# One tile form for the compressed branch and the row-maxima product, and separate PSUM banks and weight buffers for the second half's gated product

## The chip, the cores and the metric

The kernel runs on one core of one Trainium2 chip. The metric is device time in microseconds of one execution, as the median of several executions. The engines have short names here: PE is TensorE's matrix multiply and PEld its weight load, DVE is VectorE, ACT is ScalarE, POOL is GpSimd, SP is SyncE, which issues the DMA transfers.

## What is computed

One layer of a hybrid model over 1024 tokens of width 1024. Cut to what matters here:

```python
h = _rms_norm(x, norm_mix)
u = h @ w_in                      # queries, three kinds of keys and values, gates, RWKV inputs, merge gates
# attention: 8 heads in 2 groups; three branches are summed with gates:
#   compressed: 63 keys, each made of 32 tokens (mask: 16 n + 31 <= t)
#   selected:   causal over all 1024 tokens (16 blocks of 64, top 16 of 16)
#   window:     the last 512 tokens
o_nsa = gate0 * o_cmp + gate1 * o_slc + gate2 * o_win
o_rwkv = _rwkv7(...)              # a recurrence over the tokens, 8 heads
y = sig(merge0) * (o_nsa @ proj_nsa) + sig(merge1) * (o_rwkv @ proj_rwkv)
x = x + y @ w_out
x = x + _conv_ffn(_rms_norm(x, norm_ffn), ffn_up, ffn_conv, ffn_down)
```

## The kernel before

The tokens are cut into two halves of 512 columns. A dense product runs in two parts: weights and inputs are split into a high part and a rest (`whi`, `wlo`, `xhi`, `xlo`), and `mm3` adds three matmuls for each 128 input rows, 24 matmuls of 512 columns for a product of 1024 rows and 12 for one of 512. `wload` (L211) brings the weights: a DMA into `wraw`, a copy to `whi` on ACT (L216) and a subtraction to `wlo` on POOL (L217), two buffers of each. PSUM has four pairs of banks, called P, M, A and B, and `ps(tag)` takes the two of a pair in turn.

The program has four stages. (1) The input norm. (2) Attention with all projections of `u`: the attention of a head runs at its own pace, and dense products (the fillers `zproj`, `mproj`) are put between its steps, with small matmuls that prepare the RWKV part (`prelude`, L794, `loraproj`, L821). (3) The RWKV recurrence, with fillers again: the first half's `nproj`, `rproj`, `wout0`, `norm0` and `ffn0`. (4) The second half: `gated` for its eight output tiles (L1208 to L1215), then `w_out`, the norm, and the feed-forward part. A scheduler writes the order of each engine's instructions when the program is built, by priorities and its own estimate of durations; every engine then runs its list in order.

Attention of a head (`i`, `g`) goes in three steps. Row maxima are found for the three branches and put into `mx`, for all 1024 tokens. They are needed on the partitions of `q2`, beside the query's rest, so they go through a product with the identity: `M` holds, per token, three maxima and their rests, and the matmul of L500 turns 128 tokens of it into rows of PSUM. Then for each branch and half, L528 and L530 make scores with the keys on the partitions, L532 adds a mask, ACT takes the exponential twice (L537, L538), DVE the rest (L539), and L542, L545 and L547 multiply with the values. In the compressed branch the keys are 64 (63 and one empty), so its matmuls use a part of the array. Last, the finished heads are turned (L566), copied by ACT into `oT` (L568) and stored (L569).

A matmul's tile form is the part of the array that it uses, rows by columns. The trace shows it behind the tiles' names: `128*128` is the whole array, `128*64` half of its columns (64 outputs), `64*128` half of its rows (64 inputs), `64*64` a quarter.

In stage 4, `gated(m, 1, ...)` makes one 128x512 output tile: DVE multiplies the product with the gate (L652), POOL adds it to `yt` (L653), ACT and DVE split the sum into `yhi` and `ylo` (L1214, L1215). The products of `w_out` read all eight tiles of those.

## Time and profile before

| | |
|---|---|
| median of 3 runs | 1892.82 us (1892.15 to 1898.71) |
| profiled execution, its own time | 1890.38 us |
| span of the profiled execution, first to last instruction | 1888.6 us |
| PE busy | 1826.6 us (97%) |
| DVE, ACT, POOL busy | 980.8, 797.7, 655.6 us |
| attention with its fillers | about 130 to 660 us |
| the second half's gated products | 1164 to 1188 us |

How to read it: a row of the timeline gives the start of an instruction and its duration. Matmuls are pipelined, so a duration holds time in which the next ones already run; how much a matmul costs is read from one start to the next. A PE that is busy by the table can still be slowed from within.

### The profile page before, as it was taken

To read this page: it belongs to the slowest core of one execution; us is meant where nothing else is said; L and a number is where in the kernel's file an instruction comes from. 1 tells how busy PE (TensorE), PEld (TensorE's weight loads), DVE (VectorE), ACT (ScalarE), POOL (GpSimd) and SP (SyncE) were. 2 spreads that over 40 slices of the span, in tenths; PEclk is the share of its full clock that TensorE was granted. 3 is DMA by queue.
4 is the path that set the end of the run, shared out by engine and by line. 5 is a ranking of instruction groups with operands and counts; after the bars stand their busy time and mean duration, and the time that the engine had idled before them with its cause. 6 is when DMAs were issued, how large, how long until landed. Compare 5 with 4: busy or idle time off the path is not lost.

```text
span 1888.6 us, 30480 instructions
## 1 busy us (share of the span) xinstructions
PE 1826.6 (97%) x12106; PEld 1418.5 (75%) x12106; DVE 980.8 (52%) x1775; ACT 797.7 (42%) x1434; POOL 655.6 (35%) x412
## 2 busy tenths in 40 slices
PE   8999999999999999999999799999999999999998
PEld 5985656666777788777777588778888888888886
DVE  6214666767766404863443444265666553444444
ACT  5243765656566523454564443344222222222211
POOL 5212042132233434112155345756444433313220
PEclk9999999999999999899999899999999999999999
DMA  5425142232333336254544544425222211111102
GB/s 176 119 61 186 29 163 85 82 121 58 114 126 124 129 135 230 96 174 157 198 136 136 166 132 157 144 104 204 89 78 90 81 59 56 45 34 59 42 12 89
DMA packets 121342, 211.23 MB, mean 112 GB/s; under 512 B 23664, under 2 KB 52720, under 8 KB 120944
## 3 DMA queue, kind: packets, MB, share of 16 engines
q1 hardware_dynamic: 121200, 209.29, 33.4%
q8 instruction: 95, 1.56, 0.3%
q14 instruction: 47, 0.39, 0.1%
HBM read 151.00 MB, written 53.48 MB: 108 GB/s over the span
## 4 chain that ended last, share of the span: by engine, by line
PE 81%; DVE 8%; DMA 4%; issue 3%; ACT 3%; POOL 1%; SPq 0%; POOLq 0%; DVEq 0%; ACTq 0%
PE psP L223 29%; PE psA L223 12%; PE psM L223 9%; PE psP L1301 6%; PE psB L1301 6%; PE psA L528 1%; PE psA L390 1%; PE psA L530 1%; DVE pl L539 1%; PE psM L997 1%; PE psM L475 1%; DVE mp L481 1%; PE psP L821 1%; DVE hf L205 1%; PE psB L542 1%
## 5 line engine op out<-in xcount | busy, mean ns | idle before, releaser
L217 POOL TENSOR_TENSOR wlo<-wraw,whi 128x1024 fp32r<-128x1024 f32 (+1 forms) x154 | 346.6, 2252 | 577.8 <-ACT whi L216 173.0
L223 PE MATMUL psP<-hhi,whi 128*128 128x512 f32 x816 | 335.2, 412 | 16.5 <-ACT hhi L702 9.9
L223 PE MATMUL psP<-hlo,whi 128*128 128x512 f32 x816 | 330.7, 406 | 3.2 <-DVE hlo L703 1.8
L216 ACT ACTIVATE whi<-wraw 128x1024 fp32r<-128x1024 f32 (+1 forms) x154 | 152.4, 990 | 222.8 <-PE psP L223 84.7
L223 PE MATMUL psP<-hhi,wlo 128*128 128x512 f32 x816 | 215.6, 398 | 0.0
L223 PEld LDWEIGHTS psP<-hhi,whi 128*128 128x128 f32 x816 | 156.8, 193 | 56.2 <-ACT hhi L702 11.9
L223 PEld LDWEIGHTS psP<-hlo,whi 128*128 128x128 f32 x816 | 156.8, 192 | 40.4 <-DVE hlo L703 3.4
L223 PEld LDWEIGHTS psP<-hhi,wlo 128*128 128x128 f32 x816 | 152.5, 190 | 33.6 <-issue 0.7
L539 DVE TENSOR_TENSOR pl<-pf,ph 128x512 f16<-128x512 f32 (+4 forms) x208 | 123.5, 602 | 44.3 <-ACT pf L538 43.4
L537 ACT ACTIVATE ph<-psA 128x512 f16<-128x512 f32 (+4 forms) x208 | 98.8, 475 | 79.5 <-PE psA L532 57.7
L481 DVE TENSOR_REDUCE mp<-psM 128x1 f32<-128x512 f32 (+1 forms) x192 | 94.4, 513 | 42.2 <-PE psM L479 34.2
L1288 POOL TENSOR_TENSOR dl<-draw,dh 128x1024 fp32r<-128x1024 f32 x22 | 53.6, 2452 | 155.9 <-ACT dh L1287 96.7
L1265 DVE SCALAR_TENSOR_TENSOR u<-psA,par,u 128x511 f32<-128x511 f32 x64 | 47.7, 746 | 99.8 <-ACT u L1261 99.4
L538 ACT ACTIVATE pf<-psA 128x512 f32<-128x512 f32 (+4 forms) x208 | 99.3, 477 | 0.0
L1303 DVE TENSOR_TENSOR x<-x,psP 128x512 f32<-128x512 f32 x88 | 60.2, 684 | 68.1 <-PE psP L1301 67.7
L1287 ACT ACTIVATE dh<-draw 128x1024 fp32r<-128x1024 f32 x22 | 22.3, 1054 | 151.5 <-PE psB L1301 148.2
L1303 DVE TENSOR_TENSOR x<-x,psB 128x512 f32<-128x512 f32 x88 | 60.2, 684 | 45.1 <-PE psB L1301 45.1
L1265 DVE SCALAR_TENSOR_TENSOR u<-psM,par,u 128x511 f32<-128x511 f32 x64 | 47.7, 746 | 64.0 <-ACT u L1261 63.7
L1282 POOL TENSOR_TENSOR hl<-th,hh 128x1024 fp32r<-128x1024 f32 x22 | 52.8, 2402 | 74.6 <-ACT hh L1281 74.6
L542 PEld LDWEIGHTS <-ph 128*128 128x128 f16 (+1 forms) x592 | 55.7, 96 | 23.2 <-issue 10.9
L547 PEld LDWEIGHTS <-pl 128*128 128x128 f16 (+1 forms) x592 | 55.3, 98 | 22.9 <-DVE pl L539 8.0
L1301 PE MATMUL psP<-hh,dh 128*128 128x512 f32 x176 | 69.0, 392 | 2.1 <-ACT hh L1281 2.1
(377 smaller groups left out, 4254.5 us busy)
## 6 DMA issues: line engine op xcount, KB each, us to landing
wraw<-f_up SPq DMA_DIRECT2D x68, 512.0 KB, 3.2
wraw<-w_t SPq DMA_DIRECT2D x46, 512.0 KB, 3.5
draw<-f_dn SPq DMA_DIRECT2D x22, 512.0 KB, 3.2
sg_d<-zs SPq DMA_DIRECT2D x32, 256.0 KB, 2.0
wraw<-w_out SPq DMA_DIRECT2D x16, 512.0 KB, 3.3
z_d<-zs SPq DMA_DIRECT2D x28, 256.0 KB, 2.2
x<-xT SPq DMA_DIRECT2D x24, 256.0 KB, 5.8
zs<-sg_d SPq DMA_DIRECT2D x24, 256.0 KB, 3.0
```

What stands on the lines that cost most here:

```text
L216: A.activation(hi[:, :nk], raw, AF.Copy)
L217: G.tensor_sub(lo[:, :nk], raw, hi[:, :nk].bitcast(F32))
L223: T.matmul(ps, a[:, k], ks_(b, k), start=(n == 0), stop=(n == 3 * nk - 1))
L481: V.reduce_max(mp[:, x, br, t:t + 1], pm[:, 0:(b1 - b0) * 128], axis=AX.X)
L537: A.activation(ph[0:nkey, rg], pa[0:nkey, rg], AF.Exp, scale=0.125)
L538: A.activation(pf[0:nkey, rg], pa[0:nkey, rg], AF.Exp, scale=0.125)
L539: V.tensor_sub(pl[0:nkey, rg], pf[0:nkey, rg], ph[0:nkey, rg])
L542: T.matmul(pov[:, t, :], ph[0:nkey, tk], vt[0:nkey, kb, g, 0:65], start=first, stop=False, skip_group_check=True)
L547: T.matmul(pov[:, t, :], pl[0:nkey, tk], vt[0:nkey, kb, g, 0:65], start=False, stop=True, skip_group_check=True)
L1265: V.scalar_tensor_tensor(u[:, e0 + d:e0 + 512], pj[:, 0:512 - d], cw_, u[:, e0 + d:e0 + 512], op0=ALU.mult, op1=ALU.add)
L1301: T.matmul(pj, a[:, m], b[:, H[h]], start=(n == 0), stop=(n == 3 * len(hd_) - 1))
L1303: V.tensor_add(x2[m][:, H[h]], x2[m][:, H[h]], pj)
```

## The change

Three things are edited.

1. The compressed branch's keys, values, mask and scores are padded from 64 to 128 keys (`kcn`, `kch`, `kcl`, `Vc`, `k1c`, `k2c`, `mcT`, `nkey`). The padded keys are zero and masked. `M` gets 128 columns instead of 64 and holds its six columns at `oth.start`, so that L500 fills all 128 partitions of PSUM and the maxima still land where ACT reads them (L502). All matmuls of these lines then have the form 128*128. The count of instructions stays.
2. `oT` gets one buffer instead of two.
3. The second half's `gated` takes the bank pair B instead of P, and its weights come through buffers of their own (`whi`, `wlo`, `wraw` of four tiles of 128 columns, two buffers each, in the pool `op`). The first half's `gated` keeps P and the common buffers.

```diff
--- before.py
+++ after.py
@@ -118,8 +118,7 @@
     mdT = np.where(key > tok, NEG, 0.0)
     meT = np.where(key <= tok, NEG, 0.0)
     n64 = ar(64)
-    mcT = np.where(16 * n64[:, None] + 31 > ar(S)[None, :], NEG, 0.0)
-    mcT = np.concatenate([mcT, mcT], 0)
+    mcT = np.where(16 * p[:, None] + 31 > ar(S)[None, :], NEG, 0.0)
     mc = mcT[:64].T.reshape(8, 128, 64).transpose(1, 0, 2).reshape(128, 512)
     s64, t64 = p[:, None] % 64, n64[None, :]
     gm = np.concatenate([s64 < t64, s64 <= t64], 1)
@@ -208,10 +207,12 @@
 
         lastw = [None]
 
-        def wload(src, nk):
-            hi = wp.tile([128, 8, 128], FR, name="whi", bufs=2)
-            lo = wp.tile([128, 8, 128], FR, name="wlo", bufs=2)
-            raw = wp.tile([128, 8, 128], F32, name="wraw", bufs=2)[:, :nk]
+        def wload(src, nk, pool_=None):
+            t_ = pool_ or wp
+            n = nk if pool_ else 8
+            hi = t_.tile([128, n, 128], FR, name="whi", bufs=2)
+            lo = t_.tile([128, n, 128], FR, name="wlo", bufs=2)
+            raw = t_.tile([128, n, 128], F32, name="wraw", bufs=2)[:, :nk]
             lastw[0] = load(raw, src).ins
             A.activation(hi[:, :nk], raw, AF.Copy)
             G.tensor_sub(lo[:, :nk], raw, hi[:, :nk].bitcast(F32))
@@ -265,7 +266,7 @@
 
         Vs = ap_.tile([128, 8, 2, 130], F16, name="Vs")
         Vw = ap_.tile([128, 8, 2, 130], F16, name="Vw")
-        Vc = ap_.tile([64, 1, 2, 130], F16, name="Vc")
+        Vc = ap_.tile([128, 1, 2, 130], F16, name="Vc")
         G.memset(Vs[:, :, :, 64:65], 1.0)
         G.memset(Vw[:, :, :, 64:65], 1.0)
         G.memset(Vc, 0.0)
@@ -301,7 +302,7 @@
 
         WT = D["w_t"]
         kst1, kst2 = {}, {}
-        for nm, n in (("s", S), ("w", S), ("c", 64)):
+        for nm, n in (("s", S), ("w", S), ("c", 128)):
             for g in range(2):
                 kst1[nm, g] = ap_.tile([128, n], F16, name=f"k1{nm}{g}")
                 kst2[nm, g] = ap_.tile([128, n], F16, name=f"k2{nm}{g}")
@@ -334,7 +335,7 @@
                 for g in range(2):
                     for kv in range(2):
                         load(cw2[64 * g:64 * g + 64, kv, 64 * g:64 * g + 64], D["cw2"][kv])
-                kcn = tmp.tile([128, 64], F32, name="kcn")
+                kcn = tmp.tile([128, 128], F32, name="kcn")
                 G.memset(kcn, 0.0)
                 for kv in range(2):
                     for g in range(2):
@@ -363,8 +364,8 @@
                         pk = ps("A")
                         T.matmul(pk[:, 0:63], cw2[:, 0], hid, start=True, stop=True)
                         rms64(pk[:, 0:63], 63, P("gain", 1), kcn[:, 0:63], tmp)
-                        kch = tmp.tile([128, 64], F16, name="kch")
-                        kcl = tmp.tile([128, 64], F16, name="kcl")
+                        kch = tmp.tile([128, 128], F16, name="kch")
+                        kcl = tmp.tile([128, 128], F16, name="kcl")
                         V.tensor_copy(kch, kcn)
                         V.tensor_sub(kcl, kcn, kch)
                         kstack("c", 2, kch, kcl)
@@ -438,7 +439,7 @@
             yield from kphase()
             AQ["p"] = pool("attq", 1, stack=ast)
             for i in range(2):
-                m = AQ["p"].tile([128, 8, 64], F16, name=f"Mt{i}")
+                m = AQ["p"].tile([128, 8, 128], F16, name=f"Mt{i}")
                 G.memset(m, 0.0)
                 Mt.append(m)
             qproj(0, "A")
@@ -484,7 +485,7 @@
                         qproj(i + 1)
                     pm = ps("M")
                     for t in range(8):
-                        T.matmul(pm[:, t * 64:t * 64 + 64], qd[:, t * 128:t * 128 + 128], kst1["c", g],
+                        T.matmul(pm[:, t * 64:t * 64 + 64], qd[:, t * 128:t * 128 + 128], kst1["c", g][:, 0:64],
                                  start=(t == 0), stop=False, skip_group_check=True)
                     T.matmul(pm, identb, C("mc"), start=False, stop=True, skip_group_check=True)
                     V.reduce_max(mp[:, 0, 2, :], pm.rearrange("p (t n) -> p t n", n=64), axis=AX.X)
@@ -492,18 +493,19 @@
                     V.tensor_max(mx, mp[:, 0], mp[:, 1])
                     V.tensor_scalar(mx, mx, -4.0e6, -1.0 / 64, op0=ALU.max, op1=ALU.mult)
                     M = Mt[(2 * i + g) % 2]
-                    V.tensor_copy(M[:, :, 0:3], mx.rearrange("p b t -> p t b"))
-                    V.tensor_sub(M[:, :, 3:6], mx.rearrange("p b t -> p t b"), M[:, :, 0:3])
+                    mo = oth.start
+                    V.tensor_copy(M[:, :, mo:mo + 3], mx.rearrange("p b t -> p t b"))
+                    V.tensor_sub(M[:, :, mo + 3:mo + 6], mx.rearrange("p b t -> p t b"), M[:, :, mo:mo + 3])
                     for h in range(2):
                         pm = ps("M")
                         for t in range(4):
-                            T.matmul(pm[oth, t * 128:t * 128 + 128], M[:, 4 * h + t], identh, start=(t == 0),
+                            T.matmul(pm[:, t * 128:t * 128 + 128], M[:, 4 * h + t], identh, start=(t == 0),
                                      stop=(t == 3), skip_group_check=True)
                         A.activation(q2[oth, H[h]], pm[oth], AF.Copy)
 
                     for br, nm in ((0, "s"), (1, "w"), (2, "c")):
                         vt = (Vs, Vw, Vc)[br]
-                        nkey = 64 if br == 2 else 128
+                        nkey = 128
                         for h in range(2):
                             po = ps("B")
                             pov = po[:, 0:260].rearrange("p (t c) -> p t c", c=65)
@@ -518,7 +520,7 @@
                                 tg = slice(t0 * 128, t1 * 128)
                                 extra = []
                                 if br == 2:
-                                    extra.append((rg, C("mcT")[0:64, tg]))
+                                    extra.append((rg, C("mcT")[:, tg]))
                                 else:
                                     if t0 == kb:
                                         extra.append((slice((kb - b0) * 128, (kb - b0 + 1) * 128), C("mdT")))
@@ -564,7 +566,7 @@
                     pt = ps(OTAG)
                     for t in range(4):
                         T.transpose(pt[:, t * 128:t * 128 + 128], onat[:, 4 * h + t], ident)
-                    oT = AQ["p"].tile([128, 512], F32, name="oT", bufs=2)
+                    oT = AQ["p"].tile([128, 512], F32, name="oT", bufs=1)
                     A.activation(oT, pt, AF.Copy)
                     nc.sync.dma_start(onsa_d[i][:, H[h]], oT)
                     if "oT" in dbg:
@@ -643,11 +645,11 @@
                 A.activation(ob["hi"][k], t, AF.Copy)
                 V.tensor_sub(ob["lo"][k], t, ob["hi"][k].bitcast(F32))
 
-        def gated(m, h, hi, lo, s1, yt):
-            w_ = wload(D["p_rwkv"][m], 4)
+        def gated(m, h, hi, lo, s1, yt, pool_=None):
+            w_ = wload(D["p_rwkv"][m], 4, pool_)
             load(s1, sg_d[8 + m][:, H[h]])
             A.activation(s1, s1, AF.Tanh, scale=0.5)
-            pj = ps("P")
+            pj = ps("PB"[h])
             mm3(pj, w_[0], w_[1], hi, lo, 4)
             V.scalar_tensor_tensor(s1, s1, 1.0, pj, op0=ALU.add, op1=ALU.mult)
             G.tensor_add(yt, yt, s1)
@@ -1208,7 +1210,7 @@
         for m in range(8):
             yt = stage("yt")
             load(yt, np_d[1][m])
-            gated(m, 1, oh, ol, stage("s1"), yt)
+            gated(m, 1, oh, ol, stage("s1"), yt, op)
             with tc.issue_after(lastw[0]):
                 load(x2[m][:, H[1]], D["xT"][m][:, H[1]])
             A.activation(yhi[:, m], yt, AF.Copy)
```

The scheduler writes a new order. On PE, where the second half's gated products stand after the RWKV stage: before, the first half's `ffn0` products (PSUM tiles `psP`, inputs `hhi`, `hlo`) follow one another there:

```order
L223 MATMUL psP_12790<-hhi_6_12697,wlo_12784 128x512
L223 MATMUL psP_12790<-hhi_7_12698,wlo_12784 128x512
L223 MATMUL psP_12831<-hhi_0_12691,whi_12824 128x512
L223 MATMUL psP_12831<-hlo_0_12699,whi_12824 128x512
L223 MATMUL psP_12831<-hhi_1_12692,whi_12824 128x512
```

and in the changed program (its lines are one or two higher) half of a gated product (`psB`, inputs `oh`, `ol`) stands between the same two:

```order
L224 MATMUL psP_12790<-hhi_6_12697,wlo_12784 128x512
L224 MATMUL psP_12790<-hhi_7_12698,wlo_12784 128x512
L224 MATMUL psB_13413<-oh_13384,whi_13405 128x512
L224 MATMUL psB_13413<-ol_13385,whi_13405 128x512
L224 MATMUL psB_13413<-oh_13384,whi_13405 128x512
L224 MATMUL psB_13413<-ol_13385,whi_13405 128x512
L224 MATMUL psB_13413<-oh_13384,whi_13405 128x512
L224 MATMUL psB_13413<-ol_13385,whi_13405 128x512
L224 MATMUL psP_12831<-hhi_0_12691,whi_12824 128x512
```

So six of the eight gated products are spread over the rest of `ffn0`; before, all eight stood behind it. On PE at the start of `w_out`, before, the last gated product (`psP_13616`) is followed by the first products of `w_out` (`psA`, inputs `yhi`, `ylo`):

```order
L223 MATMUL psP_13616<-oh_13384,whi_13608 128x512
L223 MATMUL psP_13616<-ol_13385,whi_13608 128x512
L223 MATMUL psP_13616<-oh_13384,wlo_13609 128x512 x4
L223 MATMUL psA_13650<-yhi_13379,whi_13644 128x512
L223 MATMUL psA_13650<-ylo_13380,whi_13644 128x512
```

and in the changed program 13 matmuls of `w_out` stand ahead of the last two gated products (`psB_13587`, `psB_13616`), the rest behind them:

```order
L224 MATMUL psA_13683<-yhi_13379,whi_13677 128x512
L224 MATMUL psA_13683<-ylo_13380,whi_13677 128x512
L224 MATMUL psA_13683<-yhi_13379,whi_13677 128x512
L224 MATMUL psB_13587<-oh_13384,whi_13579 128x512
L224 MATMUL psB_13587<-ol_13385,whi_13579 128x512
L224 MATMUL psB_13587<-oh_13384,whi_13579 128x512
```

Between the last gated matmul and the first `w_out` matmul that reads its result stand 15 others then; ahead of the last two gated products no `w_out` matmul reads more than the first four of the eight tiles. On ACT at the end of the first pass (`i` = 0, two heads), before, the two copies to `oT` stand side by side:

```order
L568 ACTIVATE oT<-psA 128x512 x2
L779 ACTIVATE t_3479<-t_3479 128x512
L780 ACTIVATE t_3479<-t_3479,kbias 128x512
L537 ACTIVATE ph<-psA 128x512
L538 ACTIVATE pf<-psA 128x512
```

and in the changed program two activations of the prelude stand between them:

```order
L570 ACTIVATE oT<-psA 128x512
L781 ACTIVATE t_3479<-t_3479 128x512
L782 ACTIVATE t_3479<-t_3479,kbias 128x512
L570 ACTIVATE oT<-psA 128x512
L755 ACTIVATE t_4682<-kk 128x512
L539 ACTIVATE ph<-psA 128x512
```

For `i` = 1 and 3 other activations stood between the copies already, and for `i` = 2 the two stay side by side. Counted over the written order, neighbouring matmuls on PE differ in tile form 401 times before, 194 of them in the attention stage, and 293 times in the changed program, 86 of them in the attention stage.

## Rows read from the trace of the kernel before

**Rows 1.** The page: span.

```profile
span 1888.6 us, 30480 instructions
```

**Rows 2.** Busy us by engine (instructions), granted clock, DMA share, GB/s, by stretch.

```profile
187.00:230.00 43.00, 39.54 (x379) 26.29 (x377) 27.59 (x67) 32.57 (x67) 3.19 (x3) 0.92 0.04 14
230.00:660.00 430.00, 423.45 (x3678) 299.07 (x3677) 284.63 (x619) 258.03 (x590) 133.82 (x105) 1.00 0.34 111
1090.00:1160.00 70.00, 70.00 (x310) 57.94 (x310) 30.33 (x41) 27.05 (x46) 30.09 (x14) 1.00 0.40 129
1160.00:1200.00 40.00, 37.16 (x158) 28.77 (x157) 20.09 (x22) 16.72 (x28) 27.04 (x18) 1.00 0.62 205
```

**Rows 3.** Timeline of PE: start, duration, around a row-maxima product.

```profile
187.82 0.40 PE L223 MATMUL psP<-hlo,whi 128*128 128x512 f32 x1
188.06 0.39 PE L223 MATMUL psP<-hhi,whi 128*128 128x512 f32 x1
188.38 0.64 PE L500 MATMUL psM<-identh,Mt 128*64 128x128 f16 x8
188.94 0.50 PE L223 MATMUL psP<-hlo,whi 128*128 128x512 f32 x1
```

**Rows 4.** Timeline of PE around a compressed score product.

```profile
403.24 0.40 PE L528 MATMUL psA<-qd,k1c 128*64 128x512 f16 x1
403.48 0.38 PE L530 MATMUL psA<-q,k2c 128*64 128x512 f16 x1
403.78 0.40 PE L532 MATMUL psA<-cb,identb 64*64 64x512 bf16 x1
404.12 0.39 PE L475 MATMUL psM<-k1w,qd 128*128 128x512 f16 x1
404.34 0.22 PE L479 MATMUL psM<-cb,identb 128*128 128x128 bf16 x1
```

**Rows 5.** Timeline of PE around a compressed value product.

```profile
409.18 0.20 PE L547 MATMUL psB<-Vw,pl 128*128 128x65 f16 x1
409.31 0.20 PE L542 MATMUL psB<-Vc,ph 64*128 64x65 f16 x1
409.35 0.19 PE L545 MATMUL psB<-Vc,ph 64*128 64x64 f16 x1
409.48 0.29 PE L487 MATMUL psM<-k1c,qd 128*128 128x64 f16 x4
```

**Rows 6.** Weight loads by line: count, duration in ns (min/median/max), first and last start.

```profile
L500 PEld LDWEIGHTS <-Mt x64: 106/110/110, 188.4 to 585.5; 128*64 128x64 f16 x64
L528 PEld LDWEIGHTS <-k1s x96: 95/97/103, 150.5 to 617.1; 128*128 128x128 f16 x96
```

**Rows 7.** PE's waits from 1160 to 1205 us: total, times, longest.

```profile
PE psA L223 <- ACT whi L216: 1.4, 1, 1.4
PE psA L223 <- DVE ylo L1215: 1.0, 1, 1.0
PE psP L223 <- DVE s L652: 0.4, 1, 0.4
```

**Rows 8.** Timelines of POOL, ACT and DVE behind the last gated products.

```profile
1192.98 1.72 POOL L653 TENSOR_TENSOR yt<-yt,s 128x512 f32<-128x512 f32 x1
1194.74 0.63 ACT L1214 ACTIVATE yhi<-yt 128x512 fp32r<-128x512 f32 x1 [2.76 <-POOL yt L653]
1190.69 0.67 DVE L652 SCALAR_TENSOR_TENSOR s<-s,psP 128x512 f32<-128x512 f32 x1
```

**Rows 9.** The copies and stores of `oT` at `i` = 2; landing of all eight stores.

```profile
524.39 1.09 ACT L568 ACTIVATE oT<-psA 128x512 f32<-128x512 f32 x2
529.60 0.60 ACT L537 ACTIVATE ph<-psA 128x512 f16<-128x512 f32 x1 [4.12 <-PE psA L532]
525.73 1.01 SPq L569 DMA_DIRECT2D onsa_d<-oT  x2
DMA to landing us min/median/max: 2.0/2.3/4.2
```

## The prediction

> **What bounds the kernel now.** I read the page first, then the windows, then PE's timeline, because the windows alone mislead here. The span is 1888.6 us [rows 1] and the profiled execution took 1890.38 us, 1.8 us more. By the windows, PE is busy for 423.45 of the 430 us from 230 to 660, where most of the attention runs with its fillers; DVE has 284.63 and ACT 258.03 [rows 2]. So PE sets the pace there: fillers stand in its list wherever a head's chain would let it wait, and only 6.55 us are idle. What PE saves in this stretch comes off the time, almost whole. The stretch before, 187 to 230, is different: the first head has few fillers, PE is idle for 3.46 of 43 us.
>
> A busy PE can still lose time between two matmuls, which only the starts show. Two matmuls of 512 columns in one form start 0.22 us apart (404.12 to 404.34) [rows 4], or 0.24 for the dense product (187.82 to 188.06) [rows 3]. In the same rows the step from form `128*64` to `64*64` takes 0.30 us (403.48 to 403.78) and the step back to `128*128` takes 0.34 (403.78 to 404.12) [rows 4]: 0.08 and 0.12 more. Around the row maxima the dense product takes 0.32 until the first `128*64` matmul starts (188.06 to 188.38), 0.08 more [rows 3]. Around the value product the step to `64*128` takes 0.13 (409.18 to 409.31) and the step back 0.13 (409.35 to 409.48), where the step inside the form is 0.04 (409.31 to 409.35) [rows 5]: 0.09 more each. So a change of tile form costs PE about 0.09 to 0.10 us, on either side, for every pair of forms shown.
>
> **The change, part by part.** *One tile form.* The written order has 401 changes of form before and 293 after, so 108 go. Of the 86 that stay in attention, all but two belong to the prelude's `64*64` and the lora's `64*128` matmuls, which are not edited. 108 x 0.095 = 10.3 us. The first compressed score matmul also takes 0.24 instead of 0.22 (403.24 to 403.48) [rows 4], 16 times: 0.3 us. Together 10.6 us of PE time.
>
> What it costs elsewhere: no instruction is added. A matmul's step goes by its moving columns, and those stay (512 for the scores, 65 for the values, 128 for the maxima). ACT and DVE run over 128 partitions instead of 64 with the same elements each, so I take nothing. The larger memsets and stores of the padded tiles come once, long before the first head's use; nothing waits there. The weight loads grow from 64 to 128 columns, 96 of them (64 for `M`, 32 for the keys). The row says nothing is lost: 106 to 110 ns at 64 columns, 95 to 98 at 128 [rows 6]. I take 0; bounds: a gain of 10 ns x 96 = 1 us, and a loss if they were doubled, below.
>
> On this point a rule speaks against the change. The Trainium skill's page "TensorE: Matmul & The Clock Gate", section "LDWEIGHTS (loading the stationary operand)", gives a load time that grows with the columns, columns / 1.2 in ns; by it a load goes from 53 to 107 ns, 5.1 us for the 96, and the sum would be 5.1 us smaller if none of it lay under matmuls. The trace disagrees for these two forms, so it keeps a small chance.
>
> Of the 10.6 us not all arrives. An eighth, 1.3 us, belongs to the first head, where PE waits for others anyway [rows 2]; I count it as lost. Elsewhere PE's idle time is 1.5%, so I leave the rest: 9.3 us.
>
> *One `oT` buffer.* The second copy must now wait until the first one's store has landed, and ACT runs in order, so everything behind it waits too. The worst place is `i` = 2, where the two copies stay neighbours. The copies begin at 524.39 and take 1.09 us together, so the first is done near 525.0; its store is issued at 525.73, and stores land in 2.0 to 4.2 us, 2.3 in the median [rows 9]: at 528.0. With the second copy's 0.6 us ACT is free at 528.6, and its next instruction starts at 529.60, after 4.12 us of idle time [rows 9]. So the wait goes into ACT's idle time, with 1.0 us to spare; with the slowest store 0.9 us would be late, PE's next scores behind it. At `i` = 0, 1 and 3 the scheduler has put other work between the copies. I take 0, bound 4 x 0.9 = 3.6 us. SP stands at the second store meanwhile, and behind it a weight load; that weight is double buffered and a weight lasts for 48 dense matmuls, 11 us, against a delay of some 3.
>
> *The second half's gated products.* Before, all eight stand together, and PE waits three times there, 1.4 for `whi`, 1.0 for `ylo` and 0.4 for L652: 2.8 us [rows 7]. That is the most there is to gain. In the new order six of the eight are spread over `ffn0`, so that their DVE, POOL and ACT work runs under PE's: from 1090 to 1160 PE is busy in all 70 us while POOL has 30.09, ACT 27.05 and DVE 30.33 [rows 2]. The weights of the first two `w_out` products can be split before the last gated product; the wait for `whi` goes. What could be late next is the last tile: its chain is 0.67 on DVE, 1.72 on POOL and 0.63 on ACT, 3.0 us [rows 8], and 15 matmuls of 0.235 = 3.5 us stand between. I take 2.8, lower bound 0. The new buffers cost nothing on PE: the same matmuls in another bank.
>
> Sum: 9.3 + 0 + 2.8 = 12.1 us. From the profiled execution's 1890.38 that gives 1878.3; the median of the runs is 2.4 us above it, so against 1892.82 it is 1880.7. I forecast 1880.5 us, which is 0.65% less. About 0.5%, 9.5 us, is what a measurement of this kernel can tell from no change.
>
> **The rivals.**
> *The drains turn into waits.* If the chain through the exponentials binds as it does for the first head, PE comes earlier to matmuls whose inputs aren't ready. For it: in 187 to 230 PE idles 8% [rows 2], and the order of PE's list in the second half of attention has changed in many places. Against it: 1.5% idle elsewhere. If half of the 10.6 us is lost and half of the 2.8: 6.7 us, 1886.
>
> *Wider weights cost.* If a 64-column load took half of the 98 ns of a 128-column one, 96 loads would cost 49 ns more each, 4.7 us when bare: 12.1 - 4.7 = 7.4 us, 1885.5. Against it: the loads' own rows [rows 6]. It is the Trainium skill's rule told above, and its result is this time.
>
> *The drains stay.* If the cost came from small matmuls rather than from the form, only the second half's gain is left: 1890. Against it: inside a form the step of equally small matmuls is 0.04 [rows 5].
>
> *Slower: the spread gated products block PE.* PE runs in order, so a gated product in the middle of `ffn0` whose weights, `oh` or `ol` are late now stops the first half's work too. There are six such places, some in two or more pieces. POOL then carries two f_up weights, one gated weight and one `yt` sum per round. For it: PE did wait 1.4 us for a weight in this very part, with POOL busy 27.04 of 40 us [rows 2, 7]. Against it: in 1090 to 1160 every other engine is under half busy. To end slower than before, the six must wait more than 12.1 / 6 = 2.0 us each beyond what they gain; at 3 us each the time is 1892.8 - 9.3 + 18 = 1901.5.
>
> **How the numbers follow.** Forecast (saving 9.5 to 16 us): 0.66. Drains into waits: 0.18. Wider weights: 0.04. Drains stay: 0.05. Slower by the blocked list: 0.04. The other 0.03 is more than 16 us, if the new order removes waits that I can't see. The range 1876.5 to 1887 takes the forecast with its bounds (10.6 + 1.0 + 2.8 = 14.4 us at best, plus 2 us by which single runs differ) and the first two rivals; it leaves out the last three cases and some of the edges, near 0.2. Faster by over 0.5%: the forecast and the 0.03 above, 0.69. Within: the three rivals with a smaller gain, 0.27. Slower: 0.04.
>
> **What would show it.** In the new trace, L500, L528, L530, L532, L542, L545 and L547 (one or two lines lower) in form `128*128` alone, the steps at their edges 0.22 and 0.04 instead of 0.30 and 0.13; the attention stretch shorter by 9 us or more, with PE's idle time in it as before; no wait of PE for `whi` or `ylo` ahead of `w_out`, and `ffn0` without new waits; ACT's second `oT` copy waiting for a DMA but nobody for it. Wrong would be: PE's idle time in attention up by 4 us or more, weight loads near 200 ns, or PE waiting for `oh`, `ol` or `wlo` between 1080 and 1190.

## The result

The changed kernel takes 1879.3 us (median of 8 runs, 1874.6 to 1889.6) where the kernel before takes 1894.16 in the same series (8 runs, 1889.51 to 1900.47). The ratio is 0.9925, with a 95% interval of 0.9901 to 0.995: 14.2 us less, between 9.5 and 18.8. The forecast was 12.1 us less. The profiled execution of the changed kernel took 1885.57 us, one of the longer ones; a second profile of the same program, called "again" here, took 1879.38 us. Both are read below, because they differ in something that is not the change, the clock above all.

The windows of the first profile after the change. Columns: length, busy us by engine (instructions), granted clock, DMA share, GB/s.

```profile
193.00:236.00 43.00, 39.54 (x412) 27.94 (x412) 28.60 (x71) 33.30 (x69) 3.19 (x3) 1.00 0.04 14
236.00:666.00 430.00, 419.17 (x3675) 301.60 (x3674) 286.73 (x618) 257.76 (x590) 134.81 (x106) 0.99 0.36 115
1085.00:1155.00 70.00, 70.00 (x308) 57.62 (x307) 34.33 (x42) 30.88 (x53) 40.35 (x20) 1.00 0.57 180
1155.00:1195.00 40.00, 40.00 (x175) 32.42 (x174) 17.30 (x23) 15.96 (x26) 23.55 (x13) 1.00 0.35 112
```

They answer to [rows 2], and lie 6 us later in attention (why, below) and 5 us earlier in the second half. In the first head PE has 39.54 of 43 us before and after, but the two windows do not hold the same work (379 and 412 matmuls) or the same clock (0.92 and 1.00); the first head is cut at equal work below. In the main part of attention PE is busy for 4.3 us less in an equal window, so it waits more. In the second half's gated products it waits for nothing any more: 40.00 of 40 where it was 37.16.

To see what attention gained it has to be cut at the same work, not at the same time: from the first start of the row-maxima product (L500) to the end of the last `prelude` matmul (L794). The first of these rows is the kernel before, then after, then again.

```profile
188.38:670.78 482.40, 472.31 (x4123) 333.03 (x4122) 313.75 (x688) 293.55 (x664) 140.05 (x110) 0.99 0.32 104
```

```profile
194.44:669.19 474.75, 460.38 (x4123) 331.01 (x4122) 315.33 (x688) 292.65 (x663) 139.24 (x110) 0.99 0.33 105
```

```profile
188.82:660.02 471.20, 458.96 (x4123) 330.35 (x4122) 315.79 (x688) 292.59 (x663) 138.30 (x110) 1.00 0.33 106
```

The same 4123 matmuls take PE 472.31 us before and 460.38 after, at the same granted clock of 0.99 (6.8 us at 1.2 GHz in both): 11.9 us saved, 0.11 us for each of the 108 changes of form. The idle time (length less busy) goes from 10.1 to 14.4 us, in again to 12.2. So attention is shorter by 7.7 us in one profile and 11.2 in the other.

Not all of the 11.2 is the change: in again PE ran at 1.2 GHz for only 3.4 us of this stretch. The run `second`, described below, has the attention of the kernel before and ran all of it at 2.4 GHz. Against its row, again is 9.4 us shorter:

```profile
191.54:672.11 480.57, 469.61 (x4123) 331.53 (x4122) 312.70 (x688) 293.25 (x664) 140.16 (x110) 1.00 0.33 105
```

The first head at equal work, from its first L500 matmul to that of the second head, in `second` and in again:

```profile
191.54:231.41 39.87, 36.41 (x388) 24.69 (x387) 27.23 (x67) 31.25 (x66) 3.20 (x3) 1.00 0.04 15
188.82:227.49 38.67, 35.21 (x387) 24.52 (x387) 26.87 (x66) 30.74 (x65) 3.19 (x3) 1.00 0.05 15
```

PE idles for 3.46 us in both, and the stretch is 1.2 us shorter.

The start of attention moved because of the clock, not of the change. The stretch ahead of it, before, after and again:

```profile
0.00:188.38 188.38, 177.82 (x861) 132.40 (x861) 72.64 (x125) 75.55 (x132) 58.40 (x67) 0.99 0.44 136
```

```profile
0.00:194.44 194.44, 182.97 (x861) 134.10 (x861) 71.21 (x125) 75.45 (x132) 59.28 (x67) 0.96 0.43 132
```

```profile
0.00:188.82 188.82, 176.84 (x860) 133.98 (x861) 72.70 (x125) 75.42 (x132) 59.46 (x67) 0.99 0.44 136
```

The 861 matmuls are the same; in the first profile after the change the mean granted clock is 0.96, PE needs 5.2 us more for them, and the next execution of the same program doesn't show it. A difference of 6 us between two single profiles of this kernel says nothing until the clock is looked at.

The edges of the changed products in the timeline of PE, after. They answer to [rows 3], [rows 4] and [rows 5]:

```profile
194.20 0.40 PE L224 MATMUL psP<-hhi,whi 128*128 128x512 f32 x1
194.44 0.62 PE L502 MATMUL psM<-identh,Mt 128*128 128x128 f16 x8
...
406.50 0.38 PE L532 MATMUL psA<-q,k2c 128*128 128x512 f16 x1
406.72 0.38 PE L534 MATMUL psA<-cb,identb 128*128 128x512 bf16 x1
406.94 0.38 PE L476 MATMUL psM<-k1w,qd 128*128 128x512 f16 x1
...
411.56 0.20 PE L549 MATMUL psB<-Vw,pl 128*128 128x65 f16 x1
411.60 0.20 PE L544 MATMUL psB<-Vc,ph 128*128 128x65 f16 x1
411.63 0.20 PE L547 MATMUL psB<-Vc,ph 128*128 128x64 f16 x1
411.67 0.28 PE L488 MATMUL psM<-k1c,qd 128*128 128x64 f16 x4
```

From the dense product to the maxima 0.24 (it was 0.32), from score to mask and from mask to the next product 0.22 and 0.22 (0.30 and 0.34), around the values 0.04 and 0.04 (0.13 and 0.13). The form is `128*128` throughout.

### The profile page after: what moved, and what is told of

The parts are those of the page before. It is cut to its first block, busy times and chain, and to the rows that moved or that the text cites. A ratio compares the mean times of both kernels' runs of the same rounds, so it can differ in the third digit from the quotient of the medians.

```text
span 1883.8 us, 30458 instructions
## 1 busy us (share of the span) xinstructions
PE 1817.6 (96%) x12106; PEld 1417.4 (75%) x12106; DVE 981.5 (52%) x1775; ACT 796.1 (42%) x1434; POOL 657.7 (35%) x412
## 4 chain that ended last, share of the span: by engine, by line
PE 47%; DVE 2%; issue 2%; ACT 1%; DMA 1%; POOL 0%; POOLq 0%; SPq 0%; DVEq 0%
PE psA L224 11%; PE psP L224 10%; PE psM L224 9%; PE psP L1303 6%; PE psB L1303 6%; PE psB L224 1%; PE psA L1080 1%; DVE hf L204 0%; PE psM L999 0%; DMA zs<-x_d 0%; PE psB L1109 0%; PE psA L1096 0%; PE psM L943 0%; PE psC L1133 0%; DMA zs<-orw_d 0%
## 5 line engine op out<-in xcount | busy, mean ns | idle before, releaser
L541 DVE TENSOR_TENSOR pl<-pf,ph 128x512 f16<-128x512 f32 (+3 forms) x208 | 123.8, 604 | 44.6 <-ACT pf L540 43.7
L539 ACT ACTIVATE ph<-psA 128x512 f16<-128x512 f32 (+3 forms) x208 | 99.2, 477 | 62.0 <-PE psA L534 44.5
L540 ACT ACTIVATE pf<-psA 128x512 f32<-128x512 f32 (+3 forms) x208 | 99.9, 480 | 0.0
L544 PEld LDWEIGHTS <-ph 128*128 128x128 f16 x592 | 55.7, 96 | 23.0 <-issue 12.3
L549 PEld LDWEIGHTS <-pl 128*128 128x128 f16 x592 | 55.3, 98 | 20.6 <-issue 6.4
```

Of the source, the lines that this page charges most:

```text
L539: A.activation(ph[0:nkey, rg], pa[0:nkey, rg], AF.Exp, scale=0.125)
L540: A.activation(pf[0:nkey, rg], pa[0:nkey, rg], AF.Exp, scale=0.125)
L541: V.tensor_sub(pl[0:nkey, rg], pf[0:nkey, rg], ph[0:nkey, rg])
L544: T.matmul(pov[:, t, :], ph[0:nkey, tk], vt[0:nkey, kb, g, 0:65], start=first, stop=False, skip_group_check=True)
L549: T.matmul(pov[:, t, :], pl[0:nkey, tk], vt[0:nkey, kb, g, 0:65], start=False, stop=True, skip_group_check=True)
```

## The experiments

**The same program again.** The second profile shown above, with more timed executions.

> The changed kernel once more, to see what belongs to the program and what to one execution. Attention stretch = from the first row-maxima matmul to the last prelude matmul (482.4 us before, 474.75 in the first profile of the changed kernel); second-half stretch = from the matmul of norm0 to the first matmul that reads the second half's normed tile h2hi (228.5 and 225.4). If the gain is in the program's order: attention again 474 to 476 with 10 to 15 us of PE idle time, second half 225 to 226, and the stretch ahead of attention back near 188.4 us, because the 13.7 us of half clock there belonged to that one execution. Rival, one execution's luck: the attention stretch moves by more than 3 us between the two profiles.

1882.96 us, ratio 0.9922 (0.9894 to 0.9951). The result stands, and the stretch ahead of attention is back at 188.82 us. But attention moved by 3.55 us between the two profiles, over the 3 us that the expectation gave as the mark of one execution's luck: PE's busy time by 1.4, where the clock was down for 3.4 us less, and its idle time by 2.1. What attention gained is known to a few us, not better.

**The parts: tile forms alone, second half alone.** `form` has the first two edits (with the one `oT` buffer), `second` only the third:

```diff
-            pj = ps("P")
+            pj = ps("PB"[h])
...
-            gated(m, 1, oh, ol, stage("s1"), yt)
+            gated(m, 1, oh, ol, stage("s1"), yt, op)
```

> The tile-form edit with the single oT buffer, the second half left as before. If a change of form costs 0.095 us each: attention stretch 474 to 476 as in the changed kernel, second half 228.5 as before with the 2.8 us of waits ahead of w_out, ratio to the kernel before 0.994 to 0.996. Rival, the drains were never on the path: attention 481 to 483, ratio 0.999 to 1.001.

> Only the second half's gated product with its own banks and buffers; attention as before. If the waits ahead of w_out were all there was to gain: attention stretch 482 to 483, second half 225 to 226, ratio 0.998 to 0.999. Rival, gated products in the middle of ffn0 block PE: the second-half stretch at or above 228.5, with new waits of PE for oh, ol or weights between 1080 and 1190 us.

`form`: 0.9952 (0.9933 to 0.997), 9.1 us less. `second`: 0.9989 (0.9966 to 1.0011), 2.1 us less, not to be told from nothing by the time. Together 11.2, inside the whole change's interval. Attention in `form`:

```profile
191.87:663.32 471.45, 459.17 (x4123) 329.98 (x4122) 315.58 (x688) 292.59 (x663) 138.37 (x110) 1.00 0.33 106
```

It equals again, so the second half's edit has no part in what attention gained. It also lies below the expected 474 to 476, as again does: that forecast was taken from the first profile.

**The compressed branch alone, the row maxima alone, one `oT` buffer alone.** `branch` keeps `M` at 64 columns and `oT` at two buffers; `maxima` pads `M` alone, and needs the one `oT` buffer for room; `ot1` changes one number:

```diff
-                    oT = AQ["p"].tile([128, 512], F32, name="oT", bufs=2)
+                    oT = AQ["p"].tile([128, 512], F32, name="oT", bufs=1)
```

> The compressed branch alone is padded; M stays at 64 columns and oT keeps two buffers; the second half is as before. 92 of the 108 changes of form go. Theory (each costs 0.095 us and PE sets the pace): 92 x 0.095 = 8.7 us less PE time and about 1885, ratio 0.995. Rival (the saved PE time turns into waits in attention): half of it, 1889, ratio 0.998. Rival (the gain of the whole change came from the order that the scheduler happened to write): no change or a loss.

> Only M is padded to 128 columns, with the one oT buffer that makes room for it; the compressed branch and the second half are as before. 13 changes of form go. Theory: 13 x 0.095 = 1.2 us less, about 1892, ratio 0.999, not to be told from no change by the time; the steps at the row maxima's edges are 0.22 to 0.24 where they were 0.32. Rival (one oT buffer delays ACT): up to 3.6 us slower less 1.2, 1896.

> Only oT has one buffer instead of two. Prediction's step: ACT's second copy waits for the first one's store inside ACT's idle time, no PE wait behind it, no change (ratio 1.000). Rival: the wait is passed on to PE's next scores at each of the four places, 0.9 us each, 3.6 us slower, ratio 1.002, with PE's idle gaps behind the copies longer in the trace.

`branch`: 0.9969 (0.9948 to 0.9991), 5.9 us less. `maxima`: 0.9995 (0.9977 to 1.0013); its attention takes 480.89 us with PE busy for 469.50, where `second` has 480.57 and 469.61, so the 1.2 us expected of its 13 changes can't be told. `ot1`: 1.0003 (0.9985 to 1.0021). The stretch of attention in `branch`, and in `ot1`:

```profile
188.68:666.63 477.95, 462.91 (x4123) 332.25 (x4122) 316.70 (x688) 293.27 (x664) 139.70 (x110) 0.99 0.33 105
```

```profile
188.35:670.51 482.16, 472.00 (x4123) 332.66 (x4122) 313.99 (x688) 292.94 (x663) 139.73 (x110) 0.99 0.32 104
```

`branch` takes 9.4 us off PE's busy time for 92 changes, 0.10 each, but its idle time is 15.0 us instead of 10.1: half of the gain becomes waits. `ot1` has the idle time of before, 10.2. ACT's wait for the store is there, 4.8 us in two places, and PE has no wait for `oT` (in again one of 0.2 us):

```profile
L568 ACT ACTIVATE oT<-psA x8: 597/599/600, 302.6 to 672.1; 128x512 f32<-128x512 f32 x8
...
  DMA onsa_d<-oT: 4.8, 2
```

**The second half: the banks alone, the weight buffers alone.** `bank` is the first line of the diff of `second`, `buf` the last one with its `wload`.

> Only the second half's gated products take the bank pair B; their weights share the buffers as before. If the banks alone hold the products together (the theory that a bank of P is not free while the first half's work runs), the scheduler spreads the gated products over ffn0 and the stretch from the first half's norm to the second half's first f_up product falls from 228.5 us to about 225. If the weight buffers hold them, it stays at 228.5 and PE still waits 1.4 us for whi. Time either way within 0.2% of before.

> Only the second half's gated weights get buffers of their own; the products stay in the bank pair P. If the shared weight buffers were what made PE wait, the 1.4 us wait for whi goes and the stretch falls from 228.5 us to about 225 to 227. If the banks were, it stays at 228.5. Time either way within 0.2% of before.

Their times are those of before: 0.9996 (0.9982 to 1.001) and 1.0011 (0.9994 to 1.0027). PE's waits around the last gated products, first in `bank` (1164 to 1205 us), then in `buf` (1162 to 1203):

```profile
PE psA L223 <- ACT whi L216: 1.2, 2, 0.6
PE psA L223 <- DVE ylo L1215: 0.3, 1, 0.3
```

```profile
PE psA L225 <- ACT yhi L1216: 1.9, 1, 1.9
```

Of the 2.8 us of [rows 7] `bank` leaves 1.5 and `buf` 1.9; in `second` and after, none is left. The starts in the traces show where the products stand: in `bank` the 96 gated matmuls are still in one piece (1165.10 to 1187.64), in `buf` `w_out` matmuls split them, but none comes before 1162.51 (the last at 1188.46); only with both does the scheduler spread them over `ffn0`, from 1084.99 to 1186.30 in the first profile after. Banks and weights held them together, each by itself.

The stretch that the expectations name, from the first half's norm to the second half's first f_up product, says something else. Before, `bank`, `buf` and `second`:

```profile
1058.70:1287.23 228.53, 209.41 (x873) 166.09 (x873) 106.04 (x128) 104.18 (x162) 121.28 (x63) 0.96 0.45 146
1060.05:1286.64 226.59, 209.51 (x873) 165.87 (x873) 107.53 (x128) 103.90 (x162) 121.27 (x63) 0.96 0.45 148
1056.07:1285.50 229.43, 209.44 (x873) 166.23 (x873) 104.35 (x128) 103.27 (x162) 120.25 (x62) 0.96 0.45 146
1059.23:1283.61 224.38, 208.38 (x873) 166.45 (x873) 104.88 (x128) 102.89 (x162) 123.09 (x63) 0.96 0.45 149
```

In `ot1`, `maxima`, `branch` and `form`, whose second half is that of before, it takes 228.2 to 229.8 us. So the weight buffers alone give nothing, and the banks alone some 2 us of the 3 to 4, without any spreading. That is neither of the two outcomes that the expectation of `bank` foresaw, and it rests on one profile of each.

**What a change of form costs.** `micro` runs blocks of matmuls on ready data.

> This kernel computes none of the reference; it runs blocks of matmuls on ready data, with no waits inside a block, and its output is zeros. Blocks: full512 and full128 in form 128*128 alone, only512 and only128 in 128*64 alone, cols512 and cols128 alternating 128*128 with 128*64, rows512 and rows128 alternating 128*128 with 64*128, rowq128 alternating 64*128 with 64*64, dense in fp32r alone, mixed alternating a 512-column fp32r with a 128-column fp16 matmul in one form, mixcol the same with the fp16 one in 128*64. My theory (a change of tile form costs about 0.095 us, whatever the forms): full512 steps 0.22, only512 0.22, cols512 and rows512 0.31; full128 and only128 near 0.06, cols128, rows128 and rowq128 near 0.15; 48 of 96 such steps make the difference visible in the block's length (40 x 0.095 = 3.8 us on 8.8). Rival 1 (small matmuls cost, not the form): only128 is as slow as cols128, and cols512 steps 0.22. Rival 2 (the change of data type costs as much): mixed steps 0.09 above the sum of its two parts, and mixcol no more than mixed. Rival 3 (wider weight loads cost): a weight load of 128 columns takes twice that of 64, and full128 steps slower than only128.

Its windows, one block each (from a block's first start to the next one's): 40 matmuls of 512 columns in `128*128` alone, alternating with `128*64`, alternating with `64*128`, and `128*64` alone; 80 of 128 columns in `128*128` alone; then parts of a block of 128 columns alternating with `128*64`, of which the second is at half clock, and `128*64` alone at half clock.

```profile
14.86:23.50 8.64, 8.64 (x42) 3.92 (x40) 0.15 (x1) 0.00 (x0) 1.00 0.01 2
23.50:36.60 13.10, 13.10 (x42) 3.95 (x40) 0.15 (x1) 0.00 (x0) 1.00 0.00 0
36.60:49.42 12.82, 12.82 (x42) 3.76 (x41) 0.15 (x1) 0.00 (x0) 1.00 0.00 0
49.42:58.17 8.75, 8.75 (x41) 4.32 (x41) 0.15 (x1) 0.00 (x0) 1.00 0.00 0
58.17:62.65 4.48, 4.48 (x82) 4.48 (x81) 0.15 (x1) 0.00 (x0) 1.00 0.01 4
62.65:65.85 3.20, 3.20 (x23) 1.89 (x20) 0.15 (x1) 0.00 (x0) 1.00 0.00 0
65.95:79.75 13.80, 13.80 (x60) 6.84 (x59) 0.00 (x0) 0.00 (x0) 0.50 0.00 1
97.65:99.95 2.30, 2.30 (x23) 2.30 (x23) 0.15 (x1) 0.00 (x0) 0.50 0.00 0
```

Divided by 40: 0.216 us a step in one form, 0.328 and 0.321 when the form alternates, 0.219 in the smaller form alone. So the change costs 0.10 to 0.12, the form itself nothing. By single starts the step is 0.320 into `128*64` and 0.336 out of it; at 128 columns 0.160 and 0.176 against 0.056, so the price of 0.104 and 0.120 doesn't depend on the size. Rival 1 of that expectation falls: the part of the `128*64` block of 128 columns that ran at 2.4 GHz also steps 0.056. Rival 3 too: at 2.4 GHz 128 columns of weights load in 98 ns and 64 in 110 in the median, and full blocks step like smaller ones.

The type of the data has a price of its own. The starts of alternating fp32r (512 columns) and fp16 (128 columns), first in one form, then with the fp16 one in `128*64`:

```profile
134.34 0.48 PE L152 MATMUL mixed<-r,wr 128*128 128x512 f32 x1
134.66 0.23 PE L152 MATMUL mixed<-h,w 128*128 128x128 f16 x1
134.70 0.48 PE L152 MATMUL mixed<-r,wr 128*128 128x512 f32 x1
...
140.07 0.51 PE L152 MATMUL mixcol<-r,wr 128*128 128x512 f32 x1
140.50 0.24 PE L152 MATMUL mixcol<-h,w 128*64 128x128 f16 x1
140.68 0.49 PE L152 MATMUL mixcol<-r,wr 128*128 128x512 f32 x1
```

A pair takes 0.36 in one form and 0.61 in two, where its parts take 0.227 and 0.056 alone. So a change of type costs about 0.04 in the mean of both directions, and a change of both 0.16. Of rival 2 the first half holds (0.08 for a pair), the second doesn't: the form is the dear part. It also means that a removed change of form pays 0.12 even where the type still changes. The kernel has such changes too: in the attention stretch of again 295 neighbours differ between 32-bit and 16-bit data, at 0.04 each some 12 us by estimate, as much as the removed changes of form gave.

**One step further.** `lora` pads the `zwa` product as well (16 matmuls in `64*128`, 32 more changes of form gone), run in two series:

```diff
+                zwb = prep.tile([128, 512], F32, name="zwb", tag=("km", "kk")[h], bufs=1)
+                G.memset(zwa[64:128], 0.0)
+                G.memset(zwb[0:64], 0.0)
...
-                        T.matmul(pj, lora[kr, q // 2, jc], (zwa, zwa, zg)[q][kr], start=True, stop=True)
+                        T.matmul(pj, lora[:, q // 2, jc], (zwa, zwb, zg)[q], start=True, stop=True)
```

> The changed kernel with one more product in the full form: the lora product's two inputs of 64 rows get zero rows, in a second buffer, so that its 16 matmuls have the form 128*128; 32 of the 86 remaining changes of form in attention go. If each costs 0.095 us: 3.0 us less than the changed kernel, attention stretch 471.5 to 472.5. Rival, at these matmuls PE waits for ACT anyway (1.67 and 2.63 us in the first profile of the changed kernel): the stretch stays within 1 us of the changed kernel's and only the waits grow.

> The version with the lora product's inputs padded too, once more and with more rounds. 140 of 401 changes of form gone. Theory: 140 x 0.095 = 13.3 us of PE time, less what turns into waits in attention (4 us in the first profile of the changed kernel), plus 3.3 in the second half: ratio 0.990 to 0.993, and not slower than the changed kernel's 0.9922 to 0.9925. Rival (the saved time turns into waits as PE's other forms go): 0.993 or above.

1876.31 us, 0.9894 (0.9868 to 0.992), and 1877.06 us, 0.9911 (0.9893 to 0.9928). That is faster than the kernel before, and the lowest median of all here; its intervals overlap those of the changed kernel, so that it beats that one isn't shown. Its attention, in the first series and in the second:

```profile
186.64:661.61 474.97, 461.21 (x4126) 332.04 (x4125) 319.85 (x688) 294.19 (x663) 139.81 (x110) 0.99 0.32 105
187.12:658.84 471.72, 459.05 (x4117) 331.04 (x4125) 319.94 (x688) 293.97 (x663) 140.64 (x110) 1.00 0.33 106
```

At the same clocks the changed kernel has 474.75 (first profile) and 471.20 us (again): the stretch is within 0.6 us of it both times, as the rival said, and not the 3.0 us shorter of the theory. But the rival's reason is not seen either: PE's busy time is that of the changed kernel (460.38 and 458.96), and its idle time is 13.8 and 12.7 us for 14.4 and 12.2. Single steps around these matmuls fell as expected (0.521 to 0.429 behind, 0.148 to 0.056 ahead). Together with the stretch ahead of attention, where the second series is 1.7 us shorter than again, 1.2 us of the 3.0 remain. There are 14 more changes between 32-bit and 16-bit data (309 for 295), 0.6 us; where the rest went is open.

**Where PE waits now.** PE's waits in attention, 230 to 672 us, after:

```profile
PE psP L823 <- ACT zs L826: 2.6, 1, 2.6
PE psA L568 <- POOL mp L462: 2.0, 1, 2.0
PE psP L823 <- ACT zs L829: 1.7, 1, 1.7
```

Two of them, 4.3 us, are at the lora product: PE waits for a bank that ACT empties into `zs`, and ACT waits for the store of an earlier `zs`. This place is not new: the kernel before has 1.9 us there and `second`, with the same attention, 2.7. The wait at L568 is: it stands in after, again, `form` and `branch` (2.0, 1.2, 1.2 and 1.4 us) and neither before nor in `second`.

```profile
255.48 0.60 ACT L826 ACTIVATE zs<-psP 128x512 f32<-128x512 f32 x1 [3.99 <-DMA lw_d<-zs]
```

So `zs4` gives `zs` a fourth buffer; `M` goes back to 64 columns for the room.

```diff
-NZS = 3
+NZS = 4
...
-                m = AQ["p"].tile([128, 8, 128], F16, name=f"Mt{i}")
+                m = AQ["p"].tile([128, 8, 64], F16, name=f"Mt{i}")
```

> The changed kernel with a fourth buffer for zs; the row-maxima product goes back to 64 columns to make room for it (316 changes of form instead of 293, 23 x 0.11 = 2.5 us more PE time in attention). Theory (the new waits of PE at the lora product come from ACT's zs copy, which waits for the store of an earlier zs): with a fourth buffer ACT's waits for the stores of zs and PE's waits for zs in 230 to 672 (4.3 and 2.5 us in the two profiles) go or fall under 1 us, so that PE idles some 3 us less there; the time is about that of the changed kernel, ratio 0.992 to 0.993. Rival (the saved PE time meets the attention's own chain, whatever the buffers): PE's idle time in attention stays at 12 to 14 us, in other places, and the ratio is 0.993 to 0.995.

0.9965 (0.9949 to 0.9981): about half of the gain is gone. PE's waits in attention of `zs4`:

```profile
PE psP L822 <- ACT zs L828: 2.9, 2, 1.5
...
PE psM L476 <- DVE mp L482: 1.8, 4, 0.5
PE psM L501 <- DVE Mt L497: 1.3, 2, 0.8
```

The theory falls. The waits at the lora product are 2.9 us, neither gone nor under 1 us, and others stand around the row maxima (L476, L501). The rival fares better, but the ratio lies above its 0.993 to 0.995 too. From L500's first start to the first of L693, attention and recurrence together, again takes 860.48 us and `zs4` 867.37, at the same PE time:

```profile
188.82:1049.30 860.48, 832.99 (x7783) 630.21 (x7782) 503.10 (x1083) 470.36 (x970) 270.08 (x198) 0.98 0.39 129
```

```profile
194.19:1061.56 867.37, 832.87 (x7761) 624.84 (x7762) 513.59 (x1085) 472.98 (x972) 271.78 (x197) 0.98 0.39 128
```

The 6.9 us are idle time of PE. That the PE time agrees is chance: in `zs4` the window holds 22 matmuls fewer, 23 changes of form more, and 35.8 us at 1.2 GHz for 30.7. The scheduler wrote another order, and as `zs4` differs from the changed kernel by two edits, the buffer and the narrower `M`, which of them brought the waits isn't shown.

## Why the prediction was right

*What bounds the kernel.* Right: PE sets the pace in attention, and most of the time taken from inside its busy share came off the total. The busy share alone, 97%, would have shown no room.

*The price of a change of form.* Right in kind, a little too small: 0.11 us instead of 0.095, 11.9 us instead of 10.6. The prediction took the price from the edges in [rows 3 to 5], where one neighbour's step differs; `micro` gives 0.104 to 0.120 on clean steps. That only the form counts, not the size, is shown.

*What is lost of it.* The place was wrong. The first head lost nothing: at equal work PE idles there for 3.46 us with and without the change, and the 1.2 us saved arrive whole. Instead PE's idle time rose behind it: in the whole stretch by 4.3 us in the first profile, 2.2 in again and 4.9 in `branch`, and the mark "up by 4 us or more" was reached in the first profile. But the idle time also moves without the change, 10.1 us before and 11.0 in `second`, and against `second` again and `form` have only 1.3 us more. So the loss is between 1.3 and 4.9 us, the term was 1.3, and how far the rival "the drains turn into waits" holds stays open: half of the gain in `branch`, an eighth in again beside `second`. The one wait that only profiles with the padded branch show stands ahead of L568, 1.2 to 2.0 us. That it comes from PE being early is argued, not shown.

*Wider weights.* Free, as the row said. The loads of L502 have the 95 to 98 ns of [rows 6]:

```profile
L502 PEld LDWEIGHTS <-Mt x64: 95/98/147, 194.4 to 585.1; 128*128 128x128 f16 x64
```

The Trainium skill's rule (page "TensorE: Matmul & The Clock Gate", section "LDWEIGHTS (loading the stationary operand)") would make them twice those of 64 columns; here the 64-column ones are the slower, 110 ns in [rows 6] and in `micro` at 2.4 GHz. The measurement decides.

*One `oT` buffer.* Right: 0, by `ot1`: the time alone (1.0003, up to 1.0021) can't exclude the feared 3.6 us, its idle time, that of before, does.

*The second half.* Predicted 2.8 us. The stretch from L693's first matmul to the second half's first f_up product fell from 228.53 to 225.43 and, in again, 224.94 us: 3.1 and 3.6, and 4.2 in `second`. That is more than the 2.8 which the prediction called the most there is to gain. PE's idle time in it, where those waits lie, fell by 1.9, 2.2 and 3.1; the rest is 1.0 to 1.4 us of PE's busy time, and the clock was down for 17.1 us there instead of 20.5. The rival "the spread gated products block PE" falls: 70.00 of 70 us busy in `ffn0`. The prediction named both causes of the gain without asking whether one would do; by `bank` and `buf` it takes both to spread the products, but some 2 us of the gain came with the banks alone.

*The sum.* In again the span is 11.0 us shorter than before: 11.2 in attention and 3.6 in the second half, less 3.8 in the others: 2.0 behind `w_out` and the f_up products, where the clock was down for 6.8 us instead of 1.9, 1.4 in the recurrence, 0.9 of it idle time of PE whose cause is open, and 0.4 ahead of attention. Over the whole execution the clock was down for 59.9 us before and 58.0 in again, so little of the 11.0 us is clock. The runs say 14.2 us with an interval of 9.5 to 18.8. 12.1 lies between the two. That it lies so near is luck in part: the price of a change of form (10.6 for 11.9) and the second half were put too low, the loss was put at or below the least that the profiles show, and these errors offset each other.

## What to carry to other kernels

Read the starts of matmuls on a busy PE: the distance from start to start against that of equal neighbours shows time that no busy share shows, and padding an operand with zeros to the full tile removed it here at no price in instructions, moving columns or weight loads. Measure each place: for the lora product the same step left PE's busy time as it was. Expect a part back as waits, and look for them along the whole stretch, not only at the place of the edit; compare idle times with more than one profile, for they move by a microsecond or two without any edit. When a scheduler holds a group of products together, ask for each shared resource whether it alone would hold them: freeing one of two spread nothing and gave nothing that could be timed, though with the banks alone the stretch was 1.9 us shorter.

## What was not expected of the hardware

A change of form costs the same 0.104 and 0.120 us behind matmuls of 128 and of 512 columns. The Trainium skill's page "TensorEngine Tiling (Array Packing)", section "Key Properties", says that a change of tiling mode drains TensorE; the steps agree, and it gives no time for it. Form and type together cost 0.16 us, about the sum of 0.11 and 0.04.

The granted clock fell in `micro` in the middle of a stretch of ready work: after 4.4 us of 128-column matmuls in one form and 3.2 us of alternating ones PE went from 2.4 to 1.2 GHz, and stayed there for 34.1 us of mostly alternating matmuls. It came back while matmuls ran in `128*64` alone and fell again 6.8 us later. The alternating 512-column blocks ran at 2.4 GHz throughout. At 1.2 GHz the steps were 0.218 and 0.248 us against 0.107 in one form, so a change cost 0.11 and 0.14 there.
